# A hybrid attention and mLSTM layer: a planner's margin for side products, and where its cached values are fetched

## The chip, the cores and the metric

The kernel runs on one core of one Trainium2 chip. The metric is device time in microseconds (us), the median of several executions. A profiled execution gives a trace as well. In the trace PE is TensorE's matmuls, PEld its weight loads, DVE is VectorE, ACT is ScalarE, POOL is GpSimd, and SP (SPq) is the engine that issues the DMAs. Times of the trace count from the start of its span.

## The reference, cut to what matters

One decoder layer in fp32 for two groups that share the weights: a prompt of 512 positions and a sample group of 8 sequences with 4 new positions each (32 rows). Width 1024, FFN width 2816, 8 attention heads of 64, 4 mLSTM heads of 128.

```python
x = x + 0.5 * swiglu(rmsnorm(x), ffn1)
z = rmsnorm(x) @ w_in                      # q, k, v of attention; q, k, v, o of the mLSTM; gates
# prompt: dilated causal windows (128,1), (512,4), (2048,16), merged by their softmax denominators
# sample: the same windows over a cache of 2048 past positions and the new rows
for window, dil in ((128, 1), (512, 4), (2048, 16)):
    rows = Lb + t[:, None] - dil * j[None, :]          # j = 0 .. window // dil
    kg, vg = kc[:, rows], vc[:, rows]
    s = einsum('bthd,btjhd->bthj', q, kg) * HEAD_DIM ** -0.5
    p = exp(s - max(s)); den = sum(p)
    outs.append(einsum('bthj,btjhd->bthd', p / den, vg)); lses.append(max(s) + log(den))
att = merge_by_denominator(outs, lses)
# mLSTM, for the sample group from a given state, for the prompt from zero:
C_new = w_c * C + einsum('bhs,bshk,bshv->bhkv', w_s, k, v)
hm = rmsnorm(num / den) * sigmoid(mo)
x = x + concat(att, hm) @ w_out
x = x + 0.5 * swiglu(rmsnorm(x), ffn2)
```

Returned are x of both groups, the new keys and values, and the new mLSTM states.

## The kernel before, in words

The activations lie transposed: 8 tiles of 128 features by 544 columns (512 prompt, 32 sample). Large products run on TensorE in three passes over split operands (high and low parts in fp32r). The main work is a list of jobs; a job of the projections is 48 matmuls of 128x272 that add up in one of two PSUM slots (`mm`). The jobs are FFN 1, then 28 jobs of the input projection (`w_in`), then the output projection in two halves of eight jobs, then FFN 2. The first half of the output projection multiplies the mLSTM heads 0 to 2 (`mixed[4..6]`), the second half the attention (`mixed[0..3]`) and the last mLSTM head (`mixed[7]`).

All else in the middle stage (softmaxes, transposes, attention, mLSTM, the cache) is done by generators beside the main jobs. Their products on TensorE, the side products, write to four other PSUM banks (`aux`). The order of all instructions is written down when the program is built, by a planner, class `Order`: it keeps one clock for each engine, adds a reckoned cost for every instruction (`issue`, `tensor_engine`), and between the k steps of a job it polls the generators by priority. A generator yields a time before which it won't go on, a number of free `aux` banks that it needs, and a condition. `R(tile)` is the reckoned time at which a tile is written, plus 0.2; `done` gives a bank back at its last reckoned use. The engines then work through their queues in that fixed order and wait for one another by semaphores. So an operand that is later than reckoned stops TensorE, with all that is queued behind.

```python
    def runnable(self, h):
        if h[2] > self.t or (h[4] is not None and not h[4]()):
            return False
        return not h[3] or sum(f <= self.t for f in self.free["aux"]) >= h[3]
```

The large SBUF buffers are one ring of slots under the tag `t2` (`NT2` of them, 61), for activations, cache tiles, scores and more. A new tile takes a slot, and the instruction that first writes it waits for the slot's last readers. The planner's clocks are kept by tile name; slots are not in them. All loads and stores but a few go through SP's one queue, in the planner's order.

The sample group's attention reads the cache in tiles of 128 positions by 512 (`load_cache`, 256 KB). For each sequence there are six far tiles (`FAR`) and one near tile. The eight sequences form two groups g of four.

- `far_scores`: 48 key tiles; GpSimd multiplies each by the query rows (`pr`), VectorE reduces (`cb`). Events ("far", 0) and ("far", 1) after 24 each.
- `near_scores`: per group four near key tiles, transposed on TensorE into `kt`, then 16 products with the queries (`qd`). Event ("near", g).
- `sample_soft(g)`: waits for both events, transposes the far scores (`sx`), then softmax, then transposes the weights into `pTA` and `pTB`.
- `sample_att`: per group seven value quads (one tile of each of four sequences), each multiplied by the weights in four column groups of TensorE, added up in one bank; then the new rows (`vs`), the head selection (`c_sel`) and a copy to `attn`, from which VectorE writes the sample columns of `mixed[0..3]` (`mh`, `ml`). A quad is fetched while the one before it is in use; the first quad of all is fetched at ("far", 0).
- `ml_head(h)`: one mLSTM head. Near its end the sample states `C0` (two chunks of four sequences) are updated: `kws` by `vb` in row groups of 32 into `aux` banks, two banks for a chunk, then four VectorE operations for a chunk.

Every compute instruction but TensorE's is issued by the helper at line 223, every matmul at line 282 (`mm`), every transpose at line 287 (`tr`), so that rows of the trace are told apart by their tiles.

Of the kernel before, what the change touches and what calls it, by code (L numbers as in the profile page):

```python
# [9 lines left out]
F32R = mybir.dt.float32r  # L10
# [6 lines left out]
P = 128  # L17
# [26 lines left out]
NT2 = 61  # L44
SCORE_AHEAD = 1.5
SCORE_PRIO = 1

# [4 lines left out]
class Order:  # L52
# [4 lines left out]
    def __init__(self):  # L57
        self.t = 0.0
        self.clock = {"act": 0.0, "dve": 0.0, "pool": 0.0, "dma": 0.0, "hw": 0.0}
        self.busy, self.warm = deque(), False  # L60
        self.ready, self.used = {}, {}
        self.table = None
        self.threads = []
        self.free = {"mm": [0.0] * 2, "aux": [0.0] * 4}
        self.port = deque(maxlen=8)
# [22 lines left out]
    def resume(self, h):  # L88
        self.take("aux", h[3])
        try:  # L90
            y = next(h[5])
        except StopIteration:
            self.threads.remove(h)
            return
        y = y if isinstance(y, tuple) else (y, 0)
        h[2], h[3], h[4] = y[0], y[1], (y[2] if len(y) > 2 else None)
# [28 lines left out]
    def tensor_engine(self, at, cost):  # L125
        while self.busy and self.busy[0][1] < at - 3.4:
            self.busy.popleft()
        load = sum(b - max(a, at - 3.4) for a, b in self.busy)
        if load < 1.0:
            self.warm = False  # L130
        elif load > 3.0:
            self.warm = True
        end = at + cost * (1 if self.warm else 2)
        if self.busy and at - self.busy[-1][1] < 0.02:
            self.busy[-1][1] = end
        else:
            self.busy.append([at, end])
        return end, end
# [16 lines left out]
    def issue(self, eng, cost, outs, ins, port=False):  # L155
        at = max(self.after(self.ready, ins, eng), self.after(self.used, outs, eng))
        if eng == "pe":
            self.t, end = self.tensor_engine(max(self.t, at), cost)
        elif eng == "dma":
            self.clock["hw"] = max(self.clock["hw"], at, self.t) + (0.65 if size(outs[0]) < 1024 else 0.47)  # L160
            end = self.clock[eng] = max(self.clock[eng], self.clock["hw"] + 0.65) + cost
            end += 0.77
        else:
            at = max(self.clock[eng], at, self.t)
            if port and eng == "dve":
                for a, b in self.port:
                    at = b if a <= at < b else at
            end = self.clock[eng] = at + cost
            if port and eng == "pool":
                self.port.append((at, end))  # L170
        for a in outs:
            self.ready[a.tensor.name] = (end, eng)
        for a in list(ins) + list(outs):
            if end >= self.used.get(a.tensor.name, (0.0, ""))[0]:
                self.used[a.tensor.name] = (end, eng)
# [69 lines left out]
def hybrid_layer_kernel(ctx: ExitStack, tc: tile.TileContext, I: dict, C: dict, O: list):  # L245
# [34 lines left out]

    def mm(out, lhsT, rhs, start=True, stop=True, beside=False, **kw):
        nc.tensor.matmul(out, lhsT, rhs, start=start, stop=stop, **kw)  # L282
        n = size(rhs)
        od.issue("pe", 0.05 if beside else n / (2180.0 if rhs.dtype == F32R else 595.0), [out], [lhsT, rhs])

    def tr(out, in_, idn):
        nc.tensor.transpose(out, in_, idn)  # L287
        od.issue("pe", 0.107, [out], [in_])
# [179 lines left out]
    def spill():  # L468
        yield 0, 0, lambda: n2.n == KD
        for m in range(KD):  # L470
# [5 lines left out]
    def reload():  # L476
        yield 0, 0, lambda: at[0] >= first_out - 1
        for m in range(KD):
# [691 lines left out]
    def near_scores():  # L1170
# [10 lines left out]
        for g in range(2):  # L1181
            kts = []
            ks = [load_cache(kc, 4 * g + b4, FAR) for b4 in range(2)]
# [259 lines left out]
    def sample_att():  # L1443
# [3 lines left out]
        def prefetch(n):  # L1447
            for g, i in seq[n:n + 1]:
# [4 lines left out]
        for g in range(2):  # L1453
            o = []
            od.spawn(sample_soft(g, o), 1)
            if g == 0:
                yield 0, 0, lambda: ("far", 0) in ev
                prefetch(0)
# [5 lines left out]
            for i in range(FAR + 1):  # L1464
                prefetch(n + 1)
                n += 1
# [3 lines left out]
                for b4, v in enumerate(quad):  # L1470
                    mm(p[32 * b4:32 * b4 + 32, :], w[:, 32 * b4:32 * b4 + 32], v,
                       start=i == 0, stop=False, beside=b4 > 0, tile_position=(0, 32 * b4))
            for b4 in range(4):
                mm(p[32 * b4:32 * b4 + 32, :], pb_[0:NS, 3 * P + 32 * b4:3 * P + 32 * b4 + 32], srow["v"],
                   start=False, stop=True, beside=b4 > 0, tile_position=(0, 32 * b4))
            pmk = t2("pmk", (P, NH, HD))
# [19 lines left out]
    def ml_k(h):  # L1496
        def post(ps, full):
# [14 lines left out]
            kws = small("kws", (P, P), 3)  # L1512
# [5 lines left out]
    def ml_v(h):  # L1518
        def post(ps, full):
# [20 lines left out]
            vb = small("vb", (P, 2, V1), 3)  # L1540
# [35 lines left out]
    def ml_head(h):  # L1576
# [101 lines left out]
        dve.tensor_scalar(hS, hS, rs[:, CH:CH + 1], None, op0=OP.mult)  # L1678
        for i, c0 in enumerate(C0):
            yield R(c0) - 0.2, 2  # L1680
            pk = aux(), aux()
            for e in range(2):
                r_ = slice(2 * NS * i + NS * e, 2 * NS * i + NS * e + NS)
                mm(pk[e][:, 0:2 * V1], kws[r_], vb[r_].rearrange("p b v -> p (b v)"), beside=e > 0,
                   tile_position=(r_.start, 0))
            for b in range(HB):
                at_ = S + T * (HB * i + b) + T - 1
                dve.scalar_tensor_tensor(c0[:, b], c0[:, b], W[:, at_:at_ + 1], pk[b // 2][:, b % 2 * V1:(b % 2 + 1) * V1],
                                         op0=OP.mult, op1=OP.add)
            done(*pk)  # L1690
# [221 lines left out]
```

## Time and profile before

| | |
|---|---|
| median of 3 runs | 1129.75 us (1128.59 to 1130.44) |
| the profiled execution | 1128.2 us, span 1126.1 us |
| busy, of the span | PE 1102.5 us (98%), DVE 767.1 (68%), ACT 506.0 (45%), POOL 91.6 (8%) |
| mean granted TensorE clock | 0.996 |
| DMA | 145.36 MB, mean 129 GB/s |
| input projection's side work in the span | about 380 to 715 us |

A row of a timeline is: start, duration, engine, line, operation, output<-inputs, shapes, how many, and in brackets the idle time of that engine before it with what ended the idle time. A row of the waits is: who <- for whom, total us, times, longest. A row of the windows is: window, its length, busy us of PE, PEld, DVE, ACT and POOL (instructions in brackets), the granted TensorE clock as a share, the DMA engines' busy share, GB/s. Matmuls are pipelined, so their durations overlap; the distance of two starts tells what one costs.

### The profile page before, as it was taken

Reading aid. Unit: us, or ns where it says so; the run is one execution under the profiler, and the core shown is the slowest. Engines: PE = TensorE matmul, PEld = TensorE weight load, DVE = VectorE, ACT = ScalarE, POOL = GpSimd, SP = SyncE. Lnnn points to the kernel's source line nnn. Section 1 sums busy time; section 2 is a strip of 40 time slices with the busy share of each in tenths; the row PEclk is TensorE's granted clock in tenths of the full one; section 3 lists DMA queues with packets and bytes.
Section 4 is the critical chain, followed back from the end, with each engine's and each line's share of the span. In section 5 each row is a group of like instructions: output and inputs, shape, how many; then the busy total and the mean of one; then the engine's idle time right before and its main releaser. Section 6 shows DMA issues by size and latency. Waiting matters only on the chain. (4 is left out here: it accounts for less than half of the span.)

```text
span 1126.1 us, 21354 instructions
## 1 busy us (share of the span) xinstructions
PE 1102.5 (98%) x8807; PEld 1047.3 (93%) x8807; DVE 767.1 (68%) x1228; ACT 506.0 (45%) x905; POOL 91.6 (8%) x104
## 2 busy tenths in 40 slices
PE   7999999999999999999989999999999999999998
PEld 6999999999999989898877777999999999999998
DVE  6888337873487779699677646778962688537852
ACT  5555215451245564555544544454551355314541
POOL 0000000000000000165444010000000000000000
PEclk9999999999999999999989999999999999999999
DMA  7304312432143555676968484342233132422232
GB/s 231 101 16 158 107 38 77 148 114 78 36 140 100 162 177 138 199 214 205 277 192 264 158 279 161 104 149 76 75 124 103 51 100 76 150 76 75 66 105 60
DMA packets 143373, 145.36 MB, mean 129 GB/s; under 512 B 9013, under 2 KB 120917, under 8 KB 143277
## 3 DMA queue, kind: packets, MB, share of 16 engines
q1 hardware_dynamic: 143212, 144.01, 41.2%
q8 instruction: 69, 1.13, 0.4%
q14 instruction: 28, 0.22, 0.1%
q0 software_dynamic: 64, 0.00, 0.0%
HBM read 132.57 MB, written 9.18 MB: 126 GB/s over the span
## 5 line engine op out<-in xcount | busy, mean ns | idle before, releaser
L223 ACT CAST whi<-wraw 128x1024 fp32r<-128x1024 f32 (+3 forms) x180 | 174.0, 987 | 116.6 <-PE mm L282 86.8
L223 DVE TENSOR_TENSOR wlo<-wraw,whi 128x1024 fp32r<-128x1024 f32 (+3 forms) x180 | 206.1, 1153 | 24.8 <-ACT whi L223 24.8
L282 PE MATMUL mm<-oh,wlo 128*128 128x272 f32 x720 | 209.1, 290 | 2.2 <-DVE wlo L223 2.1
L282 PE MATMUL mm<-oh,whi 128*128 128x272 f32 x720 | 207.4, 288 | 0.1
L282 PE MATMUL mm<-ol,whi 128*128 128x272 f32 x720 | 207.2, 288 | 0.0
L282 PE MATMUL mm<-xh,whi 128*128 128x272 f32 x704 | 155.3, 302 | 0.0
L282 PE MATMUL mm<-hh,whi 128*128 128x272 f32 x704 | 147.3, 289 | 0.5 <-DVE x L223 0.5
L282 PE MATMUL mm<-xh,wlo 128*128 128x272 f32 x704 | 146.5, 290 | 0.2 <-DVE wlo L223 0.2
L282 PE MATMUL mm<-hh,wlo 128*128 128x272 f32 x704 | 146.4, 288 | 0.0
L282 PE MATMUL mm<-xl,whi 128*128 128x272 f32 x704 | 146.4, 289 | 0.0
L282 PE MATMUL mm<-hl,whi 128*128 128x272 f32 x704 | 146.4, 288 | 0.0
L282 PEld LDWEIGHTS mm<-oh,wlo 128*128 128x128 f32 x720 | 135.4, 188 | 5.5 <-DVE wlo L223 4.6
L223 DVE SCALAR_TENSOR_TENSOR x<-mm,x 128x544 f32<-128x544 f32 (+1 forms) x49 | 34.9, 713 | 154.8 <-PE mm L282 154.8
L282 PEld LDWEIGHTS mm<-oh,whi 128*128 128x128 f32 x720 | 135.5, 188 | 0.3 <-issue 0.3
L282 PEld LDWEIGHTS mm<-ol,whi 128*128 128x128 f32 x720 | 135.5, 188 | 0.0
L282 PEld LDWEIGHTS mm<-xh,whi 128*128 128x128 f32 x704 | 110.2, 190 | 12.8 <-issue 11.8
L282 PEld LDWEIGHTS mm<-xh,wlo 128*128 128x128 f32 x704 | 111.3, 190 | 0.5 <-DVE wlo L223 0.5
L282 PEld LDWEIGHTS mm<-hh,whi 128*128 128x128 f32 x704 | 110.7, 188 | 0.9 <-DVE x L223 0.8
L282 PEld LDWEIGHTS mm<-xl,whi 128*128 128x128 f32 x704 | 111.3, 190 | 0.1
L282 PEld LDWEIGHTS mm<-hh,wlo 128*128 128x128 f32 x704 | 110.8, 188 | 0.0
L282 PEld LDWEIGHTS mm<-hl,whi 128*128 128x128 f32 x704 | 110.7, 188 | 0.0
L223 ACT CAST whi<-ws 128x1024 fp32r<-128x1024 f32 x54 | 56.7, 1051 | 107.7 <-DVE ws L223 107.6
(328 smaller groups left out, 1778.5 us busy)
## 6 DMA issues: line engine op xcount, KB each, us to landing
wraw<-in_ffn_w_gate_dram SPq DMA_DIRECT2D x40, 512.0 KB
wraw<-in_ffn_w_up_dram SPq DMA_DIRECT2D x36, 512.0 KB
wraw<-in_ffn_w_down_dram SPq DMA_DIRECT2D x16, 1024.0 KB
kv<-in_cache_k_win_dram SPq DMA_DIRECT2D x56, 256.0 KB
kv<-in_cache_v_win_dram SPq DMA_DIRECT2D x56, 256.0 KB
wraw<-in_w_in_dram SPq DMA_DIRECT2D x16, 512.0 KB
wraw<-in_ffn_w_down_dram SPq DMA_DIRECT2D x8, 768.0 KB
wraw<-in_w_in_dram SPq DMA_DIRECT2D x6, 1024.0 KB
```

Of the source, the lines that this page charges most:

```text
L223: r = fn(*args, **kw)
L282: nc.tensor.matmul(out, lhsT, rhs, start=start, stop=stop, **kw)
```

## The change

- `SLACK`: from the time that the second norm's inputs are complete (`spill`) to the last job of the input projection (`reload`), a generator's step that asks for `aux` banks goes on 0.8 us later than the time it names.
- `SWITCH`: the planner adds 0.093 us to a matmul whose form (rows and columns of its weights, rounded up to 32, 64 or 128) differs from that of the one before it. No instruction is added.
- `sample_att`: the very first quad is fetched once the softmax of group 0 has been issued, and each next quad when the products of the one before it have been issued (group 1's first with group 0's last). Once all far scores are done (("far", 1)), one more quad is fetched ahead.
- `near_scores`: group 1 starts after group 0's value products (event "values").
- `ml_head`: the state update's four products go out together when four banks are free, into four banks, instead of two and two; each bank is given back after its two VectorE operations.
- One more `t2` slot (62), and two buffers instead of three for `kws` and `vb`.

```diff
 KS = float(P) ** -0.5
-NT2 = 61
+NT2 = 62
 SCORE_AHEAD = 1.5
 SCORE_PRIO = 1
+SWITCH = 0.093
+SLACK = 0.8
...
         self.clock = {"act": 0.0, "dve": 0.0, "pool": 0.0, "dma": 0.0, "hw": 0.0}
-        self.busy, self.warm = deque(), False
+        self.busy, self.warm, self.form = deque(), False, None
         self.ready, self.used = {}, {}
-        self.table = None
+        self.table, self.slack = None, 0.0
         self.threads = []
...
         y = y if isinstance(y, tuple) else (y, 0)
-        h[2], h[3], h[4] = y[0], y[1], (y[2] if len(y) > 2 else None)
+        h[2], h[3], h[4] = y[0] + (self.slack if y[1] else 0.0), y[1], (y[2] if len(y) > 2 else None)
...
-    def tensor_engine(self, at, cost):
+    def tensor_engine(self, at, cost, form):
+        if form != self.form:
+            self.form, cost = form, cost + SWITCH
         while self.busy and self.busy[0][1] < at - 3.4:
...
-    def issue(self, eng, cost, outs, ins, port=False):
+    def issue(self, eng, cost, outs, ins, port=False, form=None):
         at = max(self.after(self.ready, ins, eng), self.after(self.used, outs, eng))
         if eng == "pe":
-            self.t, end = self.tensor_engine(max(self.t, at), cost)
+            self.t, end = self.tensor_engine(max(self.t, at), cost, form)
         elif eng == "dma":
...
+    def part(n):
+        return 32 if n <= 32 else 64 if n <= 64 else P
+
     def mm(out, lhsT, rhs, start=True, stop=True, beside=False, **kw):
...
         n = size(rhs)
-        od.issue("pe", 0.05 if beside else n / (2180.0 if rhs.dtype == F32R else 595.0), [out], [lhsT, rhs])
+        od.issue("pe", 0.05 if beside else n / (2180.0 if rhs.dtype == F32R else 595.0), [out], [lhsT, rhs],
+                 False, (part(lhsT.shape[0]), part(size(lhsT))))
...
         nc.tensor.transpose(out, in_, idn)
-        od.issue("pe", 0.107, [out], [in_])
+        od.issue("pe", 0.107, [out], [in_], False, (part(in_.shape[0]), P))
...
         yield 0, 0, lambda: n2.n == KD
+        od.slack = SLACK
         for m in range(KD):
...
         yield 0, 0, lambda: at[0] >= first_out - 1
+        od.slack = 0.0
         for m in range(KD):
...
             kts = []
+            if g:
+                yield 0, 0, on("values")
             ks = [load_cache(kc, 4 * g + b4, FAR) for b4 in range(2)]
...
         def prefetch(n):
-            for g, i in seq[n:n + 1]:
+            for g, i in [x for x in seq[n:n + 1] if x not in vts]:
                 vts[(g, i)] = [load_cache(vc, 4 * g + b4, i) for b4 in range(4)]
...
             od.spawn(sample_soft(g, o), 1)
-            if g == 0:
-                yield 0, 0, lambda: ("far", 0) in ev
-                prefetch(0)
+            yield 0, 0, lambda: o
+            prefetch(n)
             yield 0, 0, lambda: o and {("v", "s", 0), ("v", "s", 1)} <= ev
...
             for i in range(FAR + 1):
-                prefetch(n + 1)
-                n += 1
+                if ("far", 1) in ev:
+                    prefetch(n + 1)
                 quad = vts.pop((g, i))
...
                        start=i == 0, stop=False, beside=b4 > 0, tile_position=(0, 32 * b4))
+                n += 1
+                prefetch(n)
             for b4 in range(4):
...
                    start=False, stop=True, beside=b4 > 0, tile_position=(0, 32 * b4))
+            ev.add("values")
             pmk = t2("pmk", (P, NH, HD))
...
             four(p, P, k[:, S:N], ident)
-            kws = small("kws", (P, P), 3)
+            kws = small("kws", (P, P), 2)
             dve.tensor_scalar(kws, p[:, 0:P], cols[:, CH, 1, h:h + 1], None, op0=OP.mult)
...
             yield R(vs) - 0.3
-            vb = small("vb", (P, 2, V1), 3)
+            vb = small("vb", (P, 2, V1), 2)
             for j in range(2):
...
         dve.tensor_scalar(hS, hS, rs[:, CH:CH + 1], None, op0=OP.mult)
+        pk = []
         for i, c0 in enumerate(C0):
-            yield R(c0) - 0.2, 2
-            pk = aux(), aux()
-            for e in range(2):
-                r_ = slice(2 * NS * i + NS * e, 2 * NS * i + NS * e + NS)
-                mm(pk[e][:, 0:2 * V1], kws[r_], vb[r_].rearrange("p b v -> p (b v)"), beside=e > 0,
-                   tile_position=(r_.start, 0))
+            if len(pk) == 2 * i:
+                yield R(*C0[i:]) - 0.2, 2
+                pk += [aux(), aux()]
+                if i == 0 and sum(f <= od.t for f in od.free["aux"]) >= 2:
+                    od.take("aux", 2)
+                    pk += [aux(), aux()]
+                for e in range(2 * i, len(pk)):
+                    r_ = slice(NS * e, NS * e + NS)
+                    mm(pk[e][:, 0:2 * V1], kws[r_], vb[r_].rearrange("p b v -> p (b v)"), beside=e > 2 * i,
+                       tile_position=(r_.start, 0))
             for b in range(HB):
                 at_ = S + T * (HB * i + b) + T - 1
-                dve.scalar_tensor_tensor(c0[:, b], c0[:, b], W[:, at_:at_ + 1], pk[b // 2][:, b % 2 * V1:(b % 2 + 1) * V1],
+                o = pk[2 * i + b // 2]
+                dve.scalar_tensor_tensor(c0[:, b], c0[:, b], W[:, at_:at_ + 1], o[:, b % 2 * V1:(b % 2 + 1) * V1],
                                          op0=OP.mult, op1=OP.add)
-            done(*pk)
+                if b % 2:
+                    done(o)
             yield R(c0) - 0.2
```

## The prediction

> **What bounds the kernel now.** I read the busy shares first, then the clock strip, then TensorE's waits, then the timelines around each long wait.
>
> ```profile
> PE 1102.5 (98%) x8807; PEld 1047.3 (93%) x8807; DVE 767.1 (68%) x1228; ACT 506.0 (45%) x905; POOL 91.6 (8%) x104
> ...
> PEclk9999999999999999999989999999999999999999
> ```
>
> TensorE is busy for 98% of the span, so only its gaps and its clock can be won. The edits touch the middle stage, between the first FFN and the output projection. These are TensorE's waits there (380 to 715 us), and the sum row of the same stretch in 5 us windows:
>
> ```profile
> PE aux L282 <- DVE aT L223: 2.2, 1, 2.2
> PE aux L287 <- DMA kv<-in_cache_k_win_dram: 1.9, 2, 1.2
> PE aux L282 <- DVE pT L223: 1.1, 1, 1.1
> PE aux L287 <- DVE vt L223: 0.8, 1, 0.8
> PE aux L287 <- DVE C L223: 0.5, 1, 0.5
> PE aux L287 <- ACT kr L223: 0.5, 1, 0.5
> PE mm L282 <- DVE x L223: 0.2, 1, 0.2
> ...
> sum 335.00, PE 327.77 PEld 282.56 DVE 245.17 ACT 169.36 POOL 90.75; mean PE 4.89 PEld 4.22 DVE 3.66 ACT 2.53 POOL 1.35
> ```
>
> The seven waits make 7.2 us, all of the idle time (335.00 - 327.77 = 7.23). The one low digit of the clock strip, in three windows of 2 us (the third number from the end is the granted clock):
>
> ```profile
> 580.00:582.00 2.00, 0.33 (x3) 0.09 (x1) 0.89 (x2) 1.31 (x2) 1.92 (x3) 0.87 0.25 60
> 582.00:584.00 2.00, 1.46 (x6) 1.46 (x7) 1.97 (x7) 0.00 (x0) 1.31 (x2) 0.50 0.67 200
> ...
> 588.00:590.00 2.00, 2.00 (x38) 1.41 (x31) 0.49 (x3) 0.00 (x0) 1.50 (x2) 0.92 0.02 8
> ```
>
> From about 581.5 to 588.3 us the clock is 0.50: a share of 0.26 of the first window (0.13 / 0.5), three whole windows at 0.50 (the first is shown) and 0.16 of the last, some 6.8 us, which cost half of that, 3.4 us. It follows these waits of TensorE:
>
> ```profile
> 572.99 1.30 PE L287 MATMUL aux<-ident,kv 128*128 128x128 f32 x8 [1.19 <-DMA kv<-in_cache_k_win_dram]
> ...
> 579.70 0.63 PE L287 MATMUL aux<-ident,kv 128*128 128x128 f32 x4 [0.69 <-DMA kv<-in_cache_k_win_dram]
> 582.54 1.23 PE L282 MATMUL aux<-vm,kw 128*128 128x129 f32 x4 [2.22 <-DVE aT L223]
> ...
> 622.33 1.09 PE L282 MATMUL aux<-pT,vr 128*64 128x128 f32 x14 [1.08 <-DVE pT L223]
> ```
>
> Behind the 2.22 and the 1.08 stand VectorE, and behind VectorE GpSimd:
>
> ```profile
> 580.45 0.69 DVE L223 TENSOR_REDUCE cb<-pr 128x8 f32<-128x512 f32 x1 [4.24 <-POOL pr L223]
> 581.79 0.69 DVE L223 TENSOR_TENSOR aT<-aux,E 128x512 f32<-128x512 f32 x1 [0.66 <-POOL pr L223]
> ...
> 617.60 0.69 DVE L223 TENSOR_REDUCE cb<-pr 128x8 f32<-128x512 f32 x1 [3.59 <-POOL pr L223]
> ```
>
> ```profile
> 579.15 2.61 POOL L223 TENSOR_TENSOR pr<-kv,qb 128x512 f32<-128x512 f32 x2 [3.84 <-PE aux L287]
> ...
> 602.39 2.50 POOL L223 TENSOR_TENSOR pr<-kv,qb 128x512 f32<-128x512 f32 x2 [2.49 <-PE aux L282]
> 616.29 1.28 POOL L223 TENSOR_TENSOR pr<-kv,qb 128x512 f32<-128x512 f32 x1 [7.88 <-PE aux L282]
> ```
>
> GpSimd's score products wait for side products of TensorE, which compute nothing for them. The shared thing is the ring of 61 large buffers (tag t2): a new product or key tile takes a slot whose last reader is a transpose of near keys (579) or a value product (602, 616). The planner reckons operands, not slots, so it cannot see this. The slots are held by these loads, on SP's queue:
>
> ```profile
> 537.55 1.90 SPq L223 DMA_DIRECT2D kv<-in_cache_v_win_dram  x4
> ...
> 565.55 6.08 SPq L223 DMA_DIRECT2D kv<-in_cache_k_win_dram  x5
> ...
> 575.34 14.14 SPq L223 DMA_DIRECT2D kv<-in_cache_k_win_dram  x7
> ```
>
> The first value quad is fetched at 537.55 and first multiplied at 601.16 (row below): four slots held for 64 us. The near keys of both groups pass through from 565 to 580, and at 575.34 SP needs 14.14 us for seven loads, against 1.90 for four.
>
> **The change part by part.**
>
> *Value quads and near scores.* The number of loads and products stays. The first quad leaves 537 us and comes after the softmax; the second group's near keys and their transposed copies (eight slots) leave 573 to 588 us and come after the first group's value products. With the 62nd slot (paid by a third buffer of kws and vb) that takes the cause from four waits: 1.19, 0.69, 2.22 and 1.08, together 5.2 us, and from the half clock, 3.4 us. Bounds: 0 (the slots stay full) and 8.6. I take 8.6, because each of these rows names a near key tile, or the GpSimd product that stands behind one or behind a value product. What is late next: the value chain, reckoned below.
>
> *Margin of 0.8 us (SLACK).* It applies only to a step that asks for PSUM banks and names a ready time, and not to a step's first start. Of the seven waits only the two on kv are of that kind. aT, C and kr are waits for a bank, vt is a first start, pT a step that asks for no bank. So by itself it is worth at most 1.9 us, counted already. Its cost: each of attention's 16 transposing steps may come 0.8 us later; a pair of heads runs two strands of two query blocks, so 4 x 2 x 0.8 = 6.4 us at most on that chain, nothing where a step waits for banks longer than that. Other products fill TensorE meanwhile.
>
> *0.093 us per change of form (SWITCH).* A number in the planner: it removes no drain. TensorE's reckoned position moves later, so every placement shifts. With the regrouping this makes new waits; the trace of before cannot show them. Bounds: 0 and 7.2 (all that the present order has); I take 3.0, the nearest rows being the 2.0 of the present waits that have nothing to do with kv (0.8 + 0.5 + 0.5 + 0.2), and a little more since all is placed anew.
>
> *State update in one group of four.* Now it is two pairs per head:
>
> ```profile
> 529.87 0.70 PE L282 MATMUL aux<-vb,kws 32*128 32x258 f32 x4
> 530.50 1.09 PE L282 MATMUL aux<-pT,vr 128*64 128x128 f32 x16
> ```
>
> A pair takes 530.50 - 529.87 = 0.63 us to the next start. Four at once, in four row groups, cost between 0.63 and 1.26; a head gains 0 to 0.63, only where four banks are free. Four heads: 0 to 2.5 us; I take 1.0, since two of the four banks are often held by attention and the value sum. The Trainium skill (TensorE: Matmul & The Clock Gate, "Measured speedup vs the span model") has row tiles overlap but for some 4 ns each; by it every head with free banks gains the whole 0.63, and the sum would be 1.5 us lower; no row of this trace has four at once with so long an operand. The pairs' updates also free a bank each as they end.
>
> *The tail.* The output projection's second half needs attention and values first:
>
> ```profile
> 601.16 1.04 PE L282 MATMUL aux<-kv,pTA 128*32 128x512 f32 x8
> ...
> 632.83 1.06 PE L282 MATMUL aux<-vs,pTB 32*32 32x512 f32 x8
> ...
> 641.09 0.88 PE L287 MATMUL aux<-ident,sx 128*128 128x128 f32 x6
> ```
>
> ```profile
> 587.28 1.58 PE L282 MATMUL aux<-kt,qd 128*32 128x132 f32 x32
> ...
> 654.43 1.04 PE L282 MATMUL aux<-kv,pTA 128*32 128x512 f32 x8
> ...
> 689.41 1.06 PE L282 MATMUL aux<-kv,pTB 128*32 128x512 f32 x8
> ...
> 692.85 0.96 PE L282 MATMUL aux<-c_sel,pmk 128*128 128x16 f32 x8
> ...
> 709.91 0.50 PE L282 MATMUL mm<-mh,whi 128*128 128x272 f32 x2
> ```
>
> ```profile
> 568.04 0.93 ACT L223 COPY sx<-cb 128x384 f32<-128x384 f32 x2 [1.71 <-PE aux L282]
> ...
> 693.85 0.21 ACT L223 COPY attn<-aux 128x64 f32<-128x64 f32 x1 [1.00 <-PE aux L282]
> ```
>
> ```profile
> 698.74 0.17 DVE L223 CAST mh<-attn 128x32 fp32r<-128x32 f32 x1
> ...
> 699.90 0.19 DVE L223 TENSOR_TENSOR ml<-attn,mh 128x32 fp32r<-128x32 f32 x1
> ```
>
> The values leave TensorE at 693.8, need 0.21 us of ACT and eight copies of VectorE in 1.35 (698.74 to 700.09), and are used at 709.91: 14.5 us of room. Added to that chain: (1) The very first quad no longer lies ready. Its load takes at least the 1.90 us of issue and at most the 7.4 from the near loads (565.55) to their first transpose (572.99); I take 5. Group 1's first quad is fetched as group 0's last is multiplied, so it lies ready as now. (2) Single fetching in group 0: seven quads now take 632.83 - 601.16 = 31.7 us, 4.5 each; at 7.4 each it would be 52. Since two are in flight again once the far scores end (616 us now, sooner without the stalls), I take +5 of 0 to 20. (3) Near scores of group 1 before its softmax: from 565.55 to 588.9 they took 23.3 us, 15.8 without 4.1 of waits and 3.4 of clock; with 2 for the copies of sx (0.93 and the steps around them), less the 8.3 that now pass from 632.83 to 641.09, +9.5 (0 to 17). (4) Group 1's six intervals take 35.0 us now beside the reload of x; that reload would be over, and at 4.5 each they take 27: -8 (or 0). Sum: 5 + 5 + 9.5 - 8 = +11.5 against 14.5 of room. The chain starts earlier by the 4.1 and 3.4 us that lie ahead of 601 (7.5), the main products by 8.6 + 1.0 - 3.0 = 6.6, so that the room stays. 3.0 us of it are left, and no wait. With all bounds low the chain gets 6 us shorter and the room is 20.6; with all high the wait is (7.4 + 20 + 17) - 14.5 = 30. The last head's chain gains from the joined update and is not in the sum.
>
> *Sum.* 1128.2 (the profiled execution; its span is 1126.1, 2.1 lie around it) - 8.6 - 1.0 + 3.0 = 1121.6. The median of the runs is 1129.75, 1.55 above that execution, so I forecast **1123.2 us**.
>
> **The rivals.**
>
> *B: the value chain becomes the bound, slower.* For it: a load's whole delay now lies in the chain, seven times in group 0, and nothing else can start the second half. Against it: 14.5 us of room. At 7.4 us per quad term (2) is 20 instead of 5, the wait 15 - 3 = 12, the time 1135.2. The kernel gets slower than before once the wait exceeds 1129.75 - 1123.2 = 6.6 us, that is with term (2) above 5 + 3.0 + 6.6 = 14.6, from (31.7 + 14.6) / 7 = 6.6 us per quad. The Trainium skill (DMA: Bandwidth & Descriptors, "Anatomy of one DMA") gives each transfer some 2.0 us that do not scale with its size, fitted for transfers issued from GpSimd; no row here parts a load's delay from its bytes. By it alone seven single quads add an estimated 14 us instead of 5, the wait is 9 - 3 = 6, and the time 1129.2.
>
> *C: it does not do what it says.* The margin reaches 1.9 of 7.2 us, one slot in 62 is little, and the quads that follow the softmax still hold slots, as at 602 and 616. Then waits and the half clock come back elsewhere: 1128.2 - 1.9 - 1.0 + 3.0 + 1.55 = 1129.9. For it: the waits at 602 and 616 come from value products, whose number stays. Against: the costliest stretch, 573 to 588 us, is emptied of eight slots.
>
> *D: all goes.* Every wait (7.2), the clock (3.4) and the joined updates (2.5), no new wait: 1128.2 - 13.1 + 1.55 = 1116.7.
>
> **How the numbers follow.** Forecast 0.50 (own range 1119 to 1127), B 0.18, C 0.22, D 0.10. A change of 0.2%, 2.3 us, is about what a measurement of this kernel tells from none: faster is below 1127.5, slower above 1132.0. Faster: 0.49 of the forecast, D's 0.10, 0.05 of C and 0.01 of B, together 0.65. Same: 0.01 of the forecast, 0.13 of C and 0.02 of B, 0.16. Slower: 0.15 of B and 0.04 of C, 0.19. Range 1117 to 1133: it takes in C and the nearer part of B, and leaves out D's far side and B's far end.
>
> **What the profile after would show.** No window of the stage below clock 1.00 and no wait on aT or kv; fewer waits of GpSimd's pr on TensorE; the kws products as x8 in one place; near products of group 1 after the first vs,pTB row. A wait of TensorE for mh or ml at the start of the second half would be B. Waits on pr, and a half clock somewhere else, would be C. The forecast fails most easily in the time per quad.

## The result, and the profile after

The changed kernel takes 1122.72 us (median of five runs, 1121.85 to 1125.39) against 1129.5 us (five runs, 1128.59 to 1130.44). The ratio of the two over their executions is 0.9949, with a 95% interval of 0.9931 to 0.9967: faster by 0.5%, which is 5.8 us of 1129.5; the two medians lie 6.8 us apart. The forecast was 1123.2 us, the range 1117 to 1133. Of the runs below, one execution each of e4 and e7 took over 1511 us at a mean clock of 0.657 and is left out of their ratios.

The profiled execution took 1125.39 us, the slowest of the five, with a span of 1123.2 us. In the helper lines, 223, 282 and 287 of before are 227, 289 and 295 now. First the busy shares and the clock strip of the changed kernel:

```profile
PE 1100.7 (98%) x8807; PEld 1046.1 (93%) x8807; DVE 768.5 (68%) x1228; ACT 507.8 (45%) x905; POOL 92.5 (8%) x104
...
PEclk9999999999999999999999999999999999999999
```

TensorE is still the bound, and the low digit of the strip is gone. TensorE's waits in the middle stage of the changed kernel, and the sum row of its windows from 380 to 715 us:

```profile
PE aux L295 <- ACT pS L227: 1.4, 1, 1.4
PE aux L295 <- DVE aTs L227: 1.0, 1, 1.0
PE aux L295 <- DVE smax L227: 0.8, 2, 0.5
PE aux L295 <- DMA kv<-in_cache_k_win_dram: 0.7, 1, 0.7
PE aux L295 <- DVE C L227: 0.6, 1, 0.6
PE aux L289 <- DVE ml L227: 0.3, 1, 0.3
PE aux L289 <- DVE Cst L227: 0.2, 1, 0.2
PE aux L289 <- DVE pT L227: 0.2, 1, 0.2
...
sum 335.00, PE 329.82 PEld 285.31 DVE 250.85 ACT 173.02 POOL 91.57; mean PE 4.92 PEld 4.26 DVE 3.74 ACT 2.58 POOL 1.37
```

The idle time is 335.00 - 329.82 = 5.2 us, against 7.2. The 2.2 us wait for aT is gone; in its place stand smaller waits in the attention of the heads (pS, aTs, smax). The clock strip hides one dip; the windows of 5 us in the changed kernel (third number from the end: granted clock), and the two TensorE rows ahead of the dip:

```profile
515.00:520.00 5.00, 3.38 (x18) 3.00 (x17) 4.44 (x11) 2.97 (x10) 1.55 (x2) 0.76 0.73 250
520.00:525.00 5.00, 4.84 (x31) 2.95 (x30) 4.86 (x17) 3.04 (x8) 1.88 (x3) 0.90 0.49 126
```

```profile
516.95 0.33 PE L295 MATMUL aux<-ident,pS 128*128 128x128 f32 x1 [1.37 <-ACT pS L227]
517.53 0.40 PE L295 MATMUL aux<-ident,pS 128*128 128x128 f32 x1 [0.25 <-DVE smax L227]
```

5 x (0.24 + 0.10) = 1.7 us are lost to the clock, half of before's 3.4, and in another place. So this execution shows 2.0 us less idle time and 1.7 us less lost to the clock, 3.7 together, of which 2.9 are seen in its span (1126.1 to 1123.2); the medians differ by more because it is the slowest of its five.

GpSimd's waits from 440 to 690 us, before and then after:

```profile
POOL pr L223 <- PE aux L282: 14.9, 3, 7.9
POOL pr L223 <- PE aux L287: 4.9, 2, 3.8
```

```profile
POOL pr L227 <- PE aux L289: 3.6, 2, 3.1
POOL pr L227 <- PE aux L295: 1.1, 2, 0.8
```

The score products waited 19.8 us on TensorE, and wait 4.7 now. The very first product is not in these sums: ahead of it GpSimd sits idle for 18 to 25 us in all the kernels, and the view puts that wait down to one engine here and another there (20.5 us to a DMA before, 24.8 to ScalarE after). The value chain of the changed kernel, in order: first quad's load, value products of group 0 (first, second, fourth, last two), the transposes of group 1's far scores (`sx`), which stand behind its near scores, group 1's value products, and the last sample columns:

```profile
579.37 2.68 SPq L227 DMA_DIRECT2D kv<-in_cache_v_win_dram  x4
```

```profile
586.47 1.07 PE L289 MATMUL aux<-kv,pTA 128*32 128x512 f32 x8
593.08 1.04 PE L289 MATMUL aux<-kv,pTA 128*32 128x512 f32 x8
...
606.29 1.06 PE L289 MATMUL aux<-kv,pTA 128*32 128x512 f32 x8
...
615.59 1.06 PE L289 MATMUL aux<-kv,pTB 128*32 128x512 f32 x8
616.58 1.06 PE L289 MATMUL aux<-vs,pTB 32*32 32x512 f32 x8
...
636.78 0.82 PE L295 MATMUL aux<-ident,sx 128*128 128x128 f32 x6
...
650.15 1.06 PE L289 MATMUL aux<-kv,pTA 128*32 128x512 f32 x8
...
671.47 1.06 PE L289 MATMUL aux<-kv,pTB 128*32 128x512 f32 x8
...
675.74 0.96 PE L289 MATMUL aux<-c_sel,pmk 128*128 128x16 f32 x8
```

```profile
678.27 0.19 DVE L227 TENSOR_TENSOR ml<-attn,mh 128x32 fp32r<-128x32 f32 x1
```

The last sample column is ready at 678.27 us, 21.6 us sooner than before (699.90), and the second half of the output projection starts at 707.05 (709.91 before). The state update was joined in one head of four; the others still show two rows of x4:

```profile
699.64 0.72 PE L289 MATMUL aux<-vb,kws 32*128 32x258 f32 x8
700.28 0.52 PE L289 MATMUL mm<-mh,whi 128*128 128x272 f32 x2
```

### The profile page after: what moved, and what is told of

The parts are those of the page before. It is cut to its first block, busy times and chain, and to the rows that moved or that the text cites. A ratio compares the mean times of both kernels' runs of the same rounds, so it can differ in the third digit from the quotient of the medians.

```text
span 1123.2 us, 21366 instructions
## 1 busy us (share of the span) xinstructions
PE 1100.7 (98%) x8807; PEld 1046.1 (93%) x8807; DVE 768.5 (68%) x1228; ACT 507.8 (45%) x905; POOL 92.5 (8%) x104
## 4 chain that ended last, share of the span: by engine, by line
PE 80%; DVE 11%; DMA 4%; ACT 3%; issue 2%; SPq 1%; POOL 0%; DVEq 0%; ACTq 0%; POOLq 0%
PE mm L289 66%; PE aux L289 10%; PE aux L295 3%; DVE wlo L227 3%; ACT whi L227 2%; DVE ws L227 1%; DMA qb<-q_d 1%; DMA wraw<-in_ffn_w_up_dram 1%; DVE wraw L227 1%; SPq L227 1%; DVE cb L227 1%; DMA kv<-in_cache_k_win_dram 1%; DMA xt<-in_x_prompt_dram 0%; DMA wraw<-in_w_in_dram 0%; DVE mo L227 0%
```

## The experiments

What is to be told apart: the ring of slots was the reason given for the waits. Is the gain that of the later fetches (fewer slots held), that of the slot added, or that of the other placements? And is it the number of slots, or only which tile happens to follow which in the ring? In the runs that change only the slots and small buffers (e2, e4 to e9), every engine's instructions stand in the same order as in the kernel that the run is made from.

All ratios are to the kernel before, measured on the same chip together with the run. "Idle" is TensorE's idle time from 380 to 715 us of the profiled execution, "clock" the sum of 5 us x (1 - granted clock) over its windows. "Clock, all" is an estimate over all executions of the kernel: 1 less their mean granted clock, times their mean span, so it takes in the ends of the span too. For the kernel before it has three values, one for each group of runs: 3.0 beside e1 to e4, 3.1 beside e5 to e8, 1.9 beside e9 to e12.

| kernel | ratio (95%) | idle | clock | clock, all | span |
|---|---|---|---|---|---|
| before, 61 slots | 1 | 7.2 | 3.4 | 1.9 to 3.1 | 1126.1 |
| e5: before, 60 slots | 1.0058 (1.0039 to 1.0077) | 12.0 | 6.8 | 6.8 | 1133.0 |
| e6: before, 61 slots, small buffers | 0.9993 (0.9982 to 1.0004) | 7.8 | 3.4 | 2.8 | 1127.6 |
| e2: before, 62 slots | 0.9953 (0.9937 to 0.9968) | 5.1 | 1.8 | 1.1 | 1123.5 |
| e7: before, 63 slots | 0.9973 (0.9958 to 0.9988) | 7.1 | 1.7 | 2.8 | 1126.7 |
| e1: before, 62 slots, new fetches | 0.9956 (0.9941 to 0.997) | 3.6 | 1.7 | 2.2 | 1120.6 |
| e3: before, margin | 0.9985 (0.9972 to 0.9997) | 7.8 | 0.0 | 1.4 | 1125.2 |
| e4: after, 60 slots | 0.9978 (0.9966 to 0.9991) | 5.8 | 0.0 | 1.7 | 1122.9 |
| e9: after, 61 slots | 0.9977 (0.9963 to 0.999) | 6.6 | 0.0 | 1.3 | 1122.3 |
| after, 62 slots | 0.9949 (0.9931 to 0.9967) | 5.2 | 1.7 | 2.0 | 1123.2 |
| e8: after, 63 slots | 0.9955 (0.9938 to 0.9972) | 5.7 | 0.0 | 1.7 | 1121.1 |
| e10: after, no margin | 1.0057 (1.004 to 1.0074) | 7.9 | 5.1 | 7.0 | 1131.3 |
| e11: after, no form cost | 0.9951 (0.9937 to 0.9965) | 3.8 | 0.0 | 1.1 | 1122.8 |
| e12: after, pairwise update | 0.9967 (0.9954 to 0.9979) | 5.2 | 0.0 | 1.1 | 1122.3 |

Span less idle less clock is 1114.2 to 1119.0 in all fourteen, so these two columns carry most of what parts the spans, from 1121 to 1133 us; the 4.8 us that are left follow neither. The ratios come from several executions, whose dips of the clock vary, so they need not follow one profile to the tenth. The clock has a large share in them: of the 6.9 us between the mean spans of e5 and before, some 3.7 are clock, and of the 4.9 us that e2 gains, some 1.9.

**The fetches with the slot (e1).** Before with the new fetch order of the values, the later near scores of group 1 and 62 slots; no margin, no form cost, the update in pairs.

```diff
-NT2 = 61
+NT2 = 62
...
-            if g == 0:
-                yield 0, 0, lambda: ("far", 0) in ev
-                prefetch(0)
+            yield 0, 0, lambda: o
+            prefetch(n)
...
+            if g:
+                yield 0, 0, on("values")
...
```

> The kernel before with the new value fetching, the later near scores and the 62nd slot alone (no margin, no form cost, old state update). Theory 1 (the gain comes from the cache tiles that no longer hold slots): 5.2 us of waits and 3.4 of half clock go, some 1.5 us of new waits come, so 1121 to 1124 us against 1129.5, and GpSimd's pr waits on TensorE fall from 19.8 us to below 8. Theory 2 (the margin does it): 1128 to 1131 us. Theory 3 (any new order redraws the waits): anywhere from 1124 to 1131, with waits of pr as before.

0.9956: nearly the whole gain of the change. No wait on aT, pT or kv stands in TensorE's list. GpSimd's waits on TensorE, from 440 to 690 us:

```profile
POOL pr L223 <- PE aux L287: 22.5, 2, 20.7
POOL pr L223 <- PE aux L282: 2.0, 2, 1.6
```

The 20.7 us are the wait ahead of the very first product, which every run has. Without it 3.8 us are left of before's 19.8, so this sign of theory 1 (below 8) is met. But the same count is no measure of the time: it is 11.5 us in e2, which is as fast, and 0.8 in e9, which is slower. What counts is whether VectorE has an instruction behind the late product that TensorE needs.

**The slot alone (e2).**

```diff
-NT2 = 61
+NT2 = 62
-            kws = small("kws", (P, P), 3)
+            kws = small("kws", (P, P), 2)
-            vb = small("vb", (P, 2, V1), 3)
+            vb = small("vb", (P, 2, V1), 2)
```

> The kernel before with 62 slots instead of 61 and nothing else; the order of every engine's instructions is the same. Theory 1: slots bind, so the waits of pr on TensorE shrink and up to 1 us of the kernel goes with them: 1127.5 to 1129.5 us. Theory 2 and theory 3: no change, within 1 us of 1129.5.

0.9953, with no instruction moved. None of the three theories had expected so much; theory 1 gave the slot up to 1 us. This one number gives what the whole change gives (0.9949), and the fetches on top of it (e1) add nothing that can be measured. The place where it works is VectorE's queue, shown here for 62 slots; with 61, aT stood behind a wait of 0.66 us on pr (row shown in the prediction):

```profile
581.51 0.69 DVE L223 TENSOR_REDUCE cb<-pr 128x8 f32<-128x512 f32 x1 [3.58 <-POOL pr L223]
582.30 0.69 DVE L223 TENSOR_TENSOR aT<-aux,E 128x512 f32<-128x512 f32 x1
```

pr is still late here (3.58 us), but only for the reduction ahead; aT follows at once, and TensorE's wait of 2.22 us is not there. Nor is the one of 1.08 for pT. A wait on kv remains, of 2.1 us.

**The margin alone (e3).**

```diff
+SLACK = 0.8
...
+        od.slack = SLACK
...
+        od.slack = 0.0
```

> The kernel before with the margin of 0.8 us alone. Theory 1: the margin reaches only the two waits on near keys (1.9 us) and moves everything else; 1126.5 to 1130 us. Theory 2: it takes most of the gain, 1122 to 1125 us, with TensorE's waits in the middle stage at 3 us or less. Theory 3: 1125 to 1131.

0.9985: 0.15%, 1.7 us. Idle time does not fall (7.8 us, now pT, mh, vt), but no window of this execution has a low clock. Over all executions the clock costs an estimated 1.4 us here and 3.0 in the kernel before beside it, so that the margin's gain by itself can be the clock's alone.

**The changed kernel with fewer slots (e4).**

```diff
-NT2 = 62
+NT2 = 60
```

> The changed kernel with 60 slots instead of 62; the order of every engine's instructions is the same. Theory 1: the changed kernel needs fewer slots in the critical stretch, so it loses little: 1 to 3 us more than 1122.7, with more waits of pr on TensorE or on ACT. Theories 2 and 3: no change, 1121.7 to 1123.7.

0.9978: 0.3% of the 0.5% are lost, with all other edits in place.

**Number or luck: before with 60 slots (e5).**

```diff
-NT2 = 61
+NT2 = 60
```

> The kernel before with 60 slots of the t2 ring in place of 61; every engine's instructions stand in the same order. Theory P (pressure: each slot fewer makes a tile wait longer for the one that held its slot): slower than before by about what one slot more gained, 4 to 6 us, so 1132 to 1134, a ratio of about 1.004, with more than 19.8 us of GpSimd products waiting on TensorE. Theory L (luck of the assignment: with another count each tile inherits another predecessor, and 61 happens to pair a GpSimd product with a late reader): no order by count; 60 may be as fast as 62, 1122 to 1127. Theory K (the gain of the run with 62 slots came from the two small buffers that went from three to two): no change, within 0.1%.

1.0058, somewhat more than theory P had. VectorE in that kernel, and TensorE's two longest waits there:

```profile
582.76 0.69 DVE L223 TENSOR_REDUCE cb<-pr 128x8 f32<-128x512 f32 x1 [5.98 <-POOL pr L223]
584.10 0.69 DVE L223 TENSOR_TENSOR aT<-aux,E 128x512 f32<-128x512 f32 x1 [0.66 <-POOL pr L223]
```

```profile
PE aux L282 <- DVE pT L223: 4.1, 1, 4.1
PE aux L282 <- DVE aT L223: 3.5, 1, 3.5
```

The wait for aT is 3.5 us with 60 slots, 2.2 with 61, and absent with 62 and 63. The same waits grow and shrink with the count from 60 to 62, as theory P has it, and GpSimd's products wait 22.2 us on TensorE (more than 19.8, as it had).

**The buffers without the slot (e6).**

```diff
-            kws = small("kws", (P, P), 3)
+            kws = small("kws", (P, P), 2)
-            vb = small("vb", (P, 2, V1), 3)
+            vb = small("vb", (P, 2, V1), 2)
```

> The kernel before with 61 slots kept and only the two small tiles kws and vb at two buffers in place of three. Theories P and L: no gain, ratio 0.999 to 1.002 (a later write of kws or vb may wait up to 1 us more). Theory K: the gain of the 62-slot run is here, ratio 0.995.

0.9993, the interval holds 1, and the wait for aT is there with its 2.2 us. Theory K falls: the slot is what counts in e2. GpSimd's products wait 22.4 us on TensorE here, as long as in e5, and yet the time is that of the kernel before.

**63 slots in both (e7, e8).**

```diff
-            vm, vs = t2("vm", (P, CH, V1)), small("vs", (P, V1), 3)
+            vm, vs = t2("vm", (P, CH, V1)), small("vs", (P, V1), 2)
...
-        hN, hS = t2("hN", (P, CH, P)), small("hS", (P, P), 2)
+        hN, hS = t2("hN", (P, CH, P)), small("hS", (P, P), 1)
...
-                cn = small("Cst", (P, V1), 5)
+                cn = small("Cst", (P, V1), 4)
...
-            dn, sq = small("dn", (P, 2), 4), small("sqj", (P, P), 2)
+            dn, sq = small("dn", (P, 2), 4), small("sqj", (P, P), 1)
```

Both have `NT2 = 63`, and e7 two buffers for kws and vb as well, as the changed kernel has.

> The kernel before with 63 slots, paid for by one buffer less of each of kws, vb, sqj, hS, vs and Cst; orders of all engines as in before. Theory P: as fast as with 62 slots or faster, ratio 0.993 to 0.996, and the GpSimd products' waits on TensorE below the 11.5 us left at 62. Theory L: anywhere from 0.994 to 1.003; slower than 62 by over 0.2% speaks for it. The smaller buffers may cost up to 1 us by themselves.

> The changed kernel with 63 slots (one buffer less of each of sqj, hS, vs and Cst), orders as in the changed kernel. Theory P: 60 slots cost it 0.3% against 62, so a 63rd brings 0 to 0.1% more: ratio to before 0.993 to 0.995, POOL products waiting on TensorE at or below 3.6 us. Theory L: 0.994 to 1.000, with a new pairing of a product and a late reader.

0.9973 and 0.9955: no better than 62 in either, and outside theory P's ranges; e7 lies 0.2% above e2, just where theory L begins. GpSimd's products wait 11.9 and 6.0 us on TensorE, not below 11.5 and 3.6. In e7 a new wait of 3.3 us for mk stands first in TensorE's list. Its trace shows the larger part of it: ahead of mk VectorE has two operations on mo, each beside a GpSimd product (from 584.28 and 586.11 us). Here they are in e7, then in e2, where at most 0.25 us of a product lies beside them:

```profile
584.46 1.70 DVE L223 TENSOR_TENSOR mo<-mo,ms 128x544 f32<-128x544 f32 x1
586.19 1.76 DVE L223 SCALAR_TENSOR_TENSOR mo<-mo,ms 128x544 f32<-128x544 f32 x1
```

```profile
584.25 0.83 DVE L223 TENSOR_TENSOR mo<-mo,ms 128x544 f32<-128x544 f32 x1 [0.22 <-ACT ms L223]
585.11 0.72 DVE L223 SCALAR_TENSOR_TENSOR mo<-mo,ms 128x544 f32<-128x544 f32 x1
```

They are 1.9 us longer in e7, of the 3.3 us. So another slot moves the products in time, and one of them can then meet VectorE at a worse place. Whether the products came at this time through the slots' new order or through the four buffers that are smaller here than in e2 wasn't separated, so the count explains 60 to 62, and what a 63rd slot alone would do stays open. e8 is no better version than the changed kernel.

**The changed kernel with before's 61 slots (e9).**

```diff
-NT2 = 62
+NT2 = 61
```

> The changed kernel with 61 slots, as many as before had; every engine's order as in the changed kernel. Theory S (substitutes: fetching values later and near keys later frees the same slots that a 62nd slot adds, and either is enough): ratio to before 0.994 to 0.996, no wait for aT over 0.5 us. Theory T (the count carries the gain: 60 slots in this kernel gave 0.9978, 62 gave 0.9949): halfway or worse, 0.9963 to 0.998, that is 1125 to 1127 us.

0.9977, theory T's side, though the wait for aT is absent, as S had it: the moves do clear that wait at 61 slots. Idle time is 1.4 us more than with 62 (6.6 against 5.2, with a wait of 2.4 for pT), and this execution is from the faster half of its twelve. All edits but the slot bring 0.80% at 60 slots (e5 to e4), 0.23% at 61 (e9) and 0.04% at 62 (e2 to the changed kernel), which can't be told from nothing; or, read the other way, from 60 to 62 slots before's order gains 1.05%, the changed order 0.29%. So the edits and the slots stand in for each other, as they would if both relieve the same ring, and with 62 slots there is little left for the edits to take. The new fetches at 61 slots without the margin and the rest were not run.

**No margin (e10).**

```diff
-SLACK = 0.8
+SLACK = 0.0
```

> The changed kernel with the margin set to zero, all else kept. Theory M (the margin's 0.15%, seen when it was put alone into the kernel before, adds to the rest): slower than the changed kernel by 1.5 to 2 us, ratio to before 0.9962 to 0.9968, with waits for pT, kv or vt of over 1 us back in the middle of the run. Theory N (the margin moved products away from the same late slots that are now free, so it has nothing left to gain): 0.994 to 0.9955.

1.0057, which neither theory had: not 0.15% but 1.1% slower than the changed kernel, and slower than before. Over its six executions the clock costs an estimated 7.0 us, against 1.9 in the kernel before beside it. TensorE's waits in that kernel, two of its windows, and the rows of the longest wait:

```profile
PE mm L289 <- ACT mh L227: 3.2, 1, 3.2
PE aux L289 <- ACT hS L227: 1.7, 1, 1.7
```

```profile
690.00:695.00 5.00, 1.75 (x9) 1.32 (x9) 3.05 (x8) 4.45 (x19) 1.95 (x2) 0.67 0.17 53
695.00:700.00 5.00, 5.00 (x29) 4.09 (x30) 3.21 (x11) 0.59 (x2) 1.26 (x2) 0.65 0.11 31
```

```profile
694.12 0.73 DVE L227 TENSOR_TENSOR ml<-hf,mh 128x544 fp32r<-128x544 f32 x1 [0.68 <-ACT mh L227]
...
706.26 0.71 DVE L227 TENSOR_TENSOR ml<-hf,mh 128x544 fp32r<-128x544 f32 x1
```

The end of head 2 slid beside that of head 3: their ml lie at 694.12 and 706.26, 12 us apart, against 679.47 and 708.63 in the changed kernel, 29 us apart. The next product in TensorE's order is one of the output projection that needs head 2's mh; TensorE idles 3.2 us for it and is then at half clock. The values are not late: the last attn column is ready at 671.08 us. e1, which has neither margin nor form cost nor joined update, is at 0.9956, so it is the margin's absence together with one of those two, or both, that makes this order, and the 1.1% are the price of this one order, not of going without a margin. Which of them wasn't tried; nor whether another small edit of the planner would place head 2 well again.

**No cost for a change of form (e11).**

```diff
-SWITCH = 0.093
+SWITCH = 0.0
```

> The changed kernel with the planner's cost for a change of the matmul's row form set to zero; another order from the first side product on. Theory M: the planned instants come too early by 0.093 us for each change of form, side products wait more often for their operands, 1 to 2 us slower than the changed kernel, ratio 0.996 to 0.997. Theory N: the 0.093 us are within what the margin covers, ratio 0.994 to 0.9955.

0.9951, theory N: with the margin in place it brings nothing that can be measured.

**The update in pairs (e12).**

```diff
-                if i == 0 and sum(f <= od.t for f in od.free["aux"]) >= 2:
-                    od.take("aux", 2)
-                    pk += [aux(), aux()]
```

(the loop as it was before, two products to a chunk)

> The changed kernel with the state update in pairs, as before. It was joined into a group of four in one head of four, and there four row tiles took 0.64 us, as long as one pair: undoing it should cost 0.6 us, ratio 0.995 to 0.996, and only the last head's rows differ. Rival: the later pair is hidden in work that is there anyway, no change, 0.9949 within 0.1%; or four accumulators held at once delay other products, and the pairs are faster by up to 1 us, 0.994.

0.9967 against 0.9949; the intervals overlap, and the 0.6 us of one joined head (0.06%) lies within them. The sign is as expected; the size is not told by this, nor is the difference itself shown.

## Why the prediction was right, and where its steps were not

The time came within 0.5 us and the likeliest case was the right one, but not every step of the sum was, and that the total agrees so closely is luck in part. In the profiled executions its terms make 2.0 us less idle time, 0.6 us for the update and, over all executions, an estimated 1.1 us of clock at most, 3.7 together, where 6.6 were forecast and the medians lie 6.8 apart; some 2 to 3 us of the gain stand in no term.

- **The cause: right.** Tiles that hold slots of the ring make a GpSimd product late, VectorE behind it, and TensorE behind that. Taking a slot away makes the waits for aT and pT longer, adding one removes both (e5, e2), with all orders unchanged. The two waits on kv are not removed by the slot (2.1 us in e2); they are gone with the new fetches (e1).
- **The cure: wrong.** The 8.6 us were credited to moving eight slots' worth of near keys and the first quad, "with the 62nd slot" as a helper, and rival C held that "one slot in 62 is little". The slot alone gave 0.47%, some 5.3 us, and the moves added nothing to it that can be measured (e1). So a ring's effect isn't in proportion to its size. That it hangs on which last reader is still in the way of one critical tile fits the rows for aT, but wasn't tested slot by slot.
- **The term of 8.6: too large.** Of its 5.2 us of waits all but 0.9 are gone (kv 0.7, pT 0.2). The half clock was taken from one execution at 3.4 us. Over all runs that list their clock, before had a mean of 0.9973 to 0.9983 and the changed kernel 0.9982; times the span that is an estimate of 1.9 to 3.1 us lost, and 2.0 us. So, by this estimate, the clock brought at most 1.1 us of the 3.4.
- **New waits of 3.0: about right.** pS 1.4, aTs 1.0, smax 0.8, ml 0.3 and Cst 0.2 make 3.7 us, and they brought a half clock of 1.7 with them.
- **The update's 1.0: the price right, the count not.** Four row tiles took 700.28 - 699.64 = 0.64 us, as long as a pair (0.63), the case in which a joined head gains all of 0.63; the Trainium skill's rule in "TensorE: Matmul & The Clock Gate", section "Measured speedup vs the span model", says that too, and this trace agrees. But four banks were free in one head only: 0.6 us, not 1.0, and not the 2.5 that the rule would give to all four.
- **The margin's bound of 1.9: the number right alone, wrong in company.** By itself it brought 1.7 us (e3). The two waits on kv are gone there, as reckoned, but others have come in their place and the idle time did not fall, so that the number agrees by luck. Without it the changed kernel is 1.1% slower (e10), though e1, which has none either, is not. The step reckoned the margin from the waits that the old trace shows; that trace could not show those that the other edits make without it.
- **The tail: too dark.** Group 0's products took 616.58 - 586.47 = 30.1 us where 36.7 were reckoned: the first four single quads came 6.6 us apart (593.08 - 586.47), the figure from which B decides, but the last three 3.1 us ((615.59 - 606.29) / 3), two in flight. The first load took 586.47 - 579.37 = 7.1 us (5 taken). Near scores of group 1: 636.78 - 616.58 = 20.2 against 8.3, +11.9 (9.5 taken). Group 1's six intervals: 671.47 - 650.15 = 21.3, -13.7 (8 taken). And the first product came 14.7 us sooner (586.47 against 601.16), where 7.5 less the 5 for its load were reckoned. Rival B is refuted with over 20 us to spare (678.27 to 707.05); the fixed cost of a transfer on which it leaned may lie in the 6.6 us, but the chain was not what TensorE waited for.

Of the signs named: no wait on aT and fewer waits of pr (19.8 to 4.7) were seen, and so were the x8 row and the later near products; a wait of 0.7 us on kv remains, and so does one low clock at another place, which had been named as a sign of rival C.

## What to carry to other kernels

When an in-order engine waits for one that computes nothing for it, look for a shared ring of buffers, and first run the kernel with one buffer more and one less, leaving all orders alone: two runs tell whether the count is a limit, and may give the gain by themselves. An edit that relieves the same limit in another way may add little to that. A planner's margin can't be priced from the old trace or from a run of it alone; take it out of the finished kernel and look at the tail, and remember that the difference then found belongs to two orders and not to the margin as such.

## What the runs showed of the hardware that was not expected

The clock's loss comes in equal pieces. In the table's column "clock" it is 0, 1.7 (in e2 1.8, by rounding), 3.4, 5.1 or 6.8 us, each piece some 3.4 us at 0.50, also after idle times well below that: 1.62 us in the changed kernel (1.37 + 0.25), 1.74 us in e10 near 508 us. Other waits as long brought none: 2.4 us for pT in e9, 1.8 in e11.

The clock records of the traces tell why. In all fourteen executions every change of the clock lies a whole number of 3.413 us after the first rise, which comes 16.4 to 23.2 us into the span. So the span can be cut into windows of 3.413 us, and a window's clock goes with TensorE's idle time in the one before it. From 380 to 715 us, all nine windows at full clock with 1.81 us idle or more were followed by one at 0.50. Those with up to 1.52 us were not, but for one with 0.99 us in e5. Of five between, at 1.55 to 1.71, two were. The window ahead of the dip in the changed kernel and the dip, then the two windows of e9 into which the edge at 518.89 us cuts its wait of 2.39 us (517.24 to 519.63):

```profile
514.18:517.60 3.42, 1.80 (x15) 1.42 (x13) 3.39 (x7) 0.98 (x4) 1.62 (x1) 1.00 1.08 338
517.60:521.01 3.41, 3.25 (x14) 2.93 (x15) 2.85 (x11) 3.00 (x8) 1.76 (x2) 0.50 0.29 106
```

```profile
515.47:518.89 3.42, 1.77 (x13) 1.55 (x13) 2.91 (x7) 3.02 (x7) 2.03 (x2) 1.00 0.42 150
518.89:522.30 3.41, 2.67 (x16) 1.74 (x17) 3.41 (x9) 1.49 (x6) 0.47 (x1) 1.00 0.50 123
```

So which wait costs a piece hangs on where the window's edges lie, and about half a window of idle time is enough. The Trainium skill ("TensorE: Matmul & The Clock Gate", section "What's actually happening") has a window of 3413 ns that runs free of the kernel, and the pieces agree with that length; it has the clock fall after an idle window of 3.4 us, and here shorter gaps were enough.

VectorE's operations with two inputs in SBUF were up to 2.6 times as long beside a GpSimd product. The two mo of e7 above are one case. In the changed kernel, first its ml of one shape (shortest, median and longest duration in ns; the longest began at 679.47 us, GpSimd's qw at 679.17), then VectorE beside three score products of GpSimd that ran from 511.54 to 515.80 us, and ScalarE behind VectorE:

```profile
L227 DVE TENSOR_TENSOR ml<-hf,mh x4: 715/721/1877, 544.4 to 708.6; 128x544 fp32r<-128x544 f32 x4
```

```profile
513.05 1.61 DVE L227 TENSOR_TENSOR rr<-rr,sg 128x544 f32<-128x544 f32 x1
514.70 1.69 DVE L227 TENSOR_TENSOR rz<-rz,rr 128x544 f32<-128x544 f32 x1
516.31 0.15 DVE L227 RECIPROCAL sden<-sden 128x2 f32<-128x2 f32 x1
```

```profile
516.49 0.69 ACT L227 ACTIVATE pS<-pS,sden 128x128 f32<-128x128 f32 x2 [2.99 <-DVE sden L227]
```

This is the chain to the longest wait that is left: at 0.72 us each, as ml has alone, rr and rz would end some 1.9 us sooner (an estimate, 1.61 + 1.69 - 2 x 0.72), sden behind them too, and by that estimate TensorE's 1.37 us for pS would not be there, nor perhaps the half clock after it. The Trainium skill ("SBUF — State Buffer", section "Who interferes with whom") has a VectorE instruction with two SBUF inputs and a GpSimd instruction that reads SBUF share a read port, where one waits for the other's whole instruction; these rows agree. The forecast had no such term, and no run here took the GpSimd products away from that place.
